# Merging two kinds of small product stages in a hybrid decoder kernel, and modelling its PSUM ring in the planner

## The chip, the cores and the metric

The kernel runs on one core of one Trainium2 chip, alone. The metric is the device time of one execution in microseconds, as the median of several runs. A profile comes from one execution on the chip. Its span goes from the first to the last instruction of that execution; its time as a run is a little longer.

## The reference, cut to what matters

Two layers of a decoder over 256 tokens of width 1024, all in fp32. A layer has one combined projection, two token mixers side by side, a gated merge, a convolution FFN and a gated embedding term:

```python
u = rms_norm(h, g_mix_norm)
qa, ka, va, qi, ki, wi, qb, kb, vb, gate_a, gate_b = split(u @ w_in)
# mixer A: 8 heads of 64, one key/value head, keys chosen by an indexer of 4 heads
rel = relu(einsum('bthd,bsd->bths', qi, ki))
iscore = where(causal, einsum('bths,bth->bts', rel, wi), -inf)
sel = top_k(iscore, 64)
o_a = softmax(qa . k_sel / 8, over valid keys) . v_sel
# mixer B: 4 heads, two softmax maps each
o_b = (softmax(q1 . k1 / 8) - lam * softmax(q2 . k2 / 8)) . vb
o_b = rms_norm(o_b, g_subln) * (1 - lam_init)
mix = sigmoid(gate_a) * (o_a @ w_branch_a) + sigmoid(gate_b) * (o_b @ w_branch_b)
h = h + mix @ w_out
h = h + conv_ffn(rms_norm(h))
h = h + sigmoid(rms_norm(h) @ w_ple_gate) * (p @ w_ple_proj)
```

The heads' queries and keys are RMS-normalised over their 64 elements (qa, ka, qb, kb) and rotated.

## The kernel before, in words

**The stream.** Every weight matrix comes in as 128 chunks of 128 x 1024 per layer, loaded by SyncE's queue into five raw buffers. ACT rounds a chunk to a high part (`split_hi`, L164) and DVE subtracts to get a low part (`split_lo`, L179; in the later part of the up-projection half of it is done on GpSimd, L175 and L176). A projection (`gemm_a`, L337 to L369) multiplies 128-row tiles of the activations, which also have a high and a low part, with both parts of the weights: three products (L361) of 512 columns for each k-step and each of the two token tiles. These products, those of the up-projection (L831, L833) and of the down-projection (L932 to L934) are most of PE's work, and they are written one after the other through the whole kernel. `prepare` (L199) splits chunks some way ahead of their use.

**The side work.** Whatever the mixers do is written as generators ("threads") and laid between the products by a planner, `Side` (L61 to L107). Each `yield` names what the stage that was just written costs on PE, DVE and ACT, in planner microseconds. `tick` (L83) is called every four token-tile steps of a projection (2.6 planner us of PE). It goes through the threads by priority, and resumes each one that is due: its last stage must be over by the planner's clocks plus a lag, DVE's clock may be at most `LIMIT_US` (3.5) ahead of PE's, and after `SIDE_US` (2) of PE time no further thread is resumed in this tick. `until` (L102) ticks with no products between, where the next product needs the side work. Then `prepare` splits further chunks. The order that the planner gives is the order of the instructions in each engine's queue; nothing is reordered by it on the chip.

**The threads of a layer.** `index_side` (L493) rotates the indexer's queries and keys, transposes them (L515, L431), and then, in one stage for each of the two query tiles i, multiplies them (L528, pairs of 64-row products, two PSUM buffers) and evicts with Relu (L531). It then spawns `select_side` (L536), which sums the heads' scores and finds the 64 largest on DVE in eight rounds (L551, L553; two rounds to a stage), which gives the mask for mixer A. `heads_side` (L568) normalises and rotates qb, kb and qa. `mixer_b` (L641) and `mixer_a` (L687) run once for each of two halves of the heads (hq) and two query tiles (i), in the orders `ORDER_B` and `ORDER_A`. A mixer's first stage is `maps` (L592): the mask is put into two PSUM buffers by an identity product (L602), the scores are added by 64-row products (L634 for B, L639 for A), DVE takes the row maxima (L607, L608), and ACT takes eight or four exponentials with their sums (L611). Then come a combination on DVE, transposes (`ptrans`, L626, L627), and the products with the values: L662 for B, which are evicted after a norm (L667 to L675), and L705 for A, four separate stages in a layer, each of which evicts to a high part (ACT, L709) and a low part (DVE, L710).

**PSUM.** Eight buffers: four for the projections (`ps_acc`, L118), and a ring of four for everything else (`ps_tp`, L119): transposes, index scores, maps, value products, and the up-projection's accumulators. A taker waits on the chip until the buffer's previous readers are done, and behind it all of PE's queue.

**Powers.** `rpow` (L260) gives (src * mul + add) ** -0.5 on GpSimd in two instructions, a tensor_scalar (L263) and a power (L264). `head_ss` (L417) squares on ACT (L420) and sums on DVE (L421).

**Between the layers.** `nxt_side` (L970) transposes and splits the first half of the new residual for the next layer while the second half's gate projection runs (`split_T_side`, L329; `split_T2`, L305, transposes at L317, evictions at L320 and L321). The residual itself is made by `gate` (L954: ACT L959, DVE L960 and L961). The next layer's `mid` (L458) does the second half.

Of the kernel before, what the change touches and what calls it, by code (L numbers as in the profile page):

```python
# [9 lines left out]
F32 = mybir.dt.float32  # L10
# [7 lines left out]
P = 128  # L18
L = 256
# [25 lines left out]
MA, MB = 0.9, 0.9  # L45
ORDER_A = [(0, 1), (1, 1), (0, 0), (1, 0)]
# [13 lines left out]

class Side:  # L61
# [6 lines left out]
    def __init__(self):  # L68
        self.threads = []
        self.pe = self.dve = self.act = 0.0  # L70

    def spawn(self, gen, prio=1):
        self.threads.append([prio, gen, 0.0])
        self.threads.sort(key=lambda t: t[0])
# [8 lines left out]
    def tick(self):  # L83
        start = self.pe
        for t in list(self.threads):
            if t[2] > self.pe or self.dve > self.pe + LIMIT_US or self.pe > start + SIDE_US:
                continue
            try:
                pe, dve, act = next(t[1])
            except StopIteration:  # L90
                self.threads.remove(t)
                continue
            self.pe += pe
            end = self.pe
            if dve:
# [14 lines left out]
def decoder_kernel(ctx: ExitStack, tc: tile.TileContext, x, xa, pT, ws, fc, tb, gf, rope, out):  # L110
# [149 lines left out]
    def rpow(dst, src, mul, add):  # L260
        n = src.shape[-1]
        t = sm.tile([P, 8], F32, name="pw", bufs=4)
        nc.gpsimd.tensor_scalar(t[:, :n], src, mul, add, op0=ALU.mult, op1=ALU.add)  # L263
        nc.gpsimd.tensor_tensor(dst, t[:, :n], mhalf[:, :n], op=ALU.pow)  # L264
# [18 lines left out]
    def b4(name, dt=F32):  # L283
        return blk.tile([P, 4, L], dt, tag="blk", name=name)

# [19 lines left out]
    def split_T2(srcs, hf, k0, scale, x, between=None, first=0):  # L305
# [5 lines left out]
        for a in range(0, 2, n):  # L311
            pt = ps_tp.tile([P, 2, L], F32, name="tp")[:, :n, :]
# [104 lines left out]
    def head_ss(src, n):  # L417
        sq = sm.tile([P, 8, 64], F32, name="sq", **T2)[:, :n, :]
        ss = sm.tile([P, 8], F32, name="hss", bufs=3)
        nc.scalar.activation(sq, src, AF.Square)  # L420
        nc.vector.reduce_sum(ss[:, :n], sq, axis=AX.X)  # L421
        return ss[:, :n]

    def transposed(srcs, nb, dst):

        for b0 in range(0, nb, 2):
            n = min(2, nb - b0)
            pt = ps_tp.tile([P, 2, L], F32, name="tp")
# [19 lines left out]
    for l in range(DEPTH):  # L448
# [44 lines left out]
        def index_side(pi):  # L493
            kk, iq, wvs = [], [], []
            for i in range(2):
# [6 lines left out]
                rpow(rk, head_ss(v[:, 0:64].unsqueeze(1), 1), 1.0 / 64, EPS)  # L502
# [9 lines left out]
            pt = ps_tp.tile([P, 2, L], F32, name="tp")  # L512
# [9 lines left out]
            for i in range(2):  # L522
                S = P * (i + 1)
                rel = b4("rel")[:, :, :S]
                ps = [ps_tp.tile([P, 2, L], F32, name="tp") for _ in range(2)]
# [7 lines left out]
                yield 0.85 * (i + 1), 0.0, 0.9  # L533
# [34 lines left out]
        def heads_side(pr, nm, is_q):  # L568

            rows, rq = [], []  # L570
            for i in range(2):
# [4 lines left out]
                if is_q:  # L576
                    rope_rows(q3, v, 8, rt[nm], i)
                    rpow(r_, head_ss(v, 8), 1.0, 64 * EPS)
                else:
                    rpow(r_, head_ss(v, 8), 1.0 / 64, EPS)  # L580
# [11 lines left out]
        def maps(qn, product, i, hq, mk):  # L592
# [6 lines left out]
            pss = [ps_tp.tile([P, 2, L], F32, name="tp") for _ in range(2)]  # L599
# [16 lines left out]
        def ptrans(src, nh, i):  # L616
# [4 lines left out]
            for a in range(0, n, 4):  # L621
                w = min(4, n - a)
                pt = ps_tp.tile([P, 4, P], F32, name="tp")
# [17 lines left out]
        def mixer_b(hq, i):  # L641
            while not {"qb", "kb"} <= flags:
                yield NONE
            pe, sums = maps("qb", product_b, i, hq, cmb)
            yield 0.9 + 0.9 * i, 0.8 + 0.6 * i, MA + MB * i
# [429 lines left out]
```

## Time and profile before

| what | value |
|---|---|
| time, median of 3 runs | 789.85 us (788.91 to 790.34) |
| the profiled execution's own time | 788.69 us |
| its span, first to last instruction | 786.9 us |
| around the span | 1.8 us |
| granted TensorE clock, mean over the span | 0.999 of full speed |
| PE matmul instructions | 4034 |
| read from HBM | 138.22 MB |

The profiled execution lies 0.2 us below the fastest of the three runs shown and 1.16 us below their median. In the profile, PE is TensorE's products, PEld its weight loads (which overlap them), DVE is VectorE, ACT ScalarE, POOL GpSimd and SP SyncE. A product's end in the trace is modelled and overlaps its successor's start, so the starts of successive products are what shows PE's pace; a merged row of a timeline gives the start of its first and the end of its last instruction. "Idle before" and its releaser stand in square brackets.

### The profile page before, as it was taken

The numbers are of one execution on the slowest core, as the hardware profiler recorded it, in microseconds if no ns is written. First come the engines' busy times: TensorE is split into PE (matmuls) and PEld (weight loads), VectorE is DVE, ScalarE is ACT, GpSimd is POOL, SyncE is SP. The second block draws the span as 40 slices with busy tenths as digits, with TensorE's granted clock in tenths as the row PEclk, the third lists the DMA queues.
The fourth block names the chain that finished last, engine by engine and source line by source line (L and its number), as shares of the span: only waits on it lengthen the run. The fifth ranks groups of instructions, "written<-read, shape, count | busy, mean of one in ns | idle before, by whom it ended". The sixth has DMA issues, their size and how long they took to land.

```text
span 786.9 us, 11698 instructions
## 1 busy us (share of the span) xinstructions
PE 779.7 (99%) x4034; PEld 648.1 (82%) x4034; DVE 588.6 (75%) x1128; ACT 501.3 (64%) x886; POOL 162.7 (21%) x162
## 2 busy tenths in 40 slices
PE   9999999999999999999999999999999999999997
PEld 7877886788888888888888778778888888888886
DVE  5987997675887778754687889768668878795643
ACT  5776657455877777553576486565468777773541
POOL 0250300001344442000123213000104444400000
PEclk9999999999999999999999999999999999999999
DMA  9654353462665556656465345445636656558521
GB/s 331 229 174 152 123 193 125 149 228 94 213 211 180 198 192 210 229 162 224 134 195 177 125 142 166 147 135 189 209 119 207 204 176 202 180 180 290 172 96 54
DMA packets 40204, 140.04 MB, mean 178 GB/s; under 512 B 4560, under 2 KB 5200, under 8 KB 40144
## 3 DMA queue, kind: packets, MB, share of 16 engines
q1 hardware_dynamic: 39280, 137.44, 52.8%
q10 hardware_dynamic: 864, 1.84, 0.7%
q8 instruction: 32, 0.52, 0.3%
q14 instruction: 28, 0.23, 0.1%
HBM read 138.22 MB, written 1.05 MB: 177 GB/s over the span
## 4 chain that ended last, share of the span: by engine, by line
PE 91%; DVE 3%; ACT 3%; POOL 1%; issue 1%; DVEq 0%; ACTq 0%
PE acc L361 36%; PE tp L831 21%; PE tp L833 11%; PE acc L932 5%; PE acc L934 5%; PE acc L933 5%; ACT pe L611 2%; PE tp L317 2%; DVE wl L179 2%; PE tp L626 1%; PE tp L705 1%; PE tp L662 1%; PE tp L639 1%; POOL rq L264 1%; PE tp L431 1%
## 5 line engine op out<-in xcount | busy, mean ns | idle before, releaser
L164 ACT ACTIVATE wh<-raw 128x1024 fp32r<-128x1024 f32 x254 | 263.9, 1057 | 38.4 <-PE acc L934 23.4
L179 DVE TENSOR_TENSOR wl<-raw,wh 128x1024 fp32r<-128x1024 f32 x178 | 213.8, 1220 | 27.8 <-ACT wh L164 27.5
L361 PE MATMUL acc<-wh,u 128*128 128x512 f32 (+1 forms) x672 | 215.1, 394 | 0.0
L831 PE MATMUL tp<-u,wh 128*128 128x512 f32 x704 | 177.1, 392 | 0.0
L361 PEld LDWEIGHTS acc<-wh,u 128*128 128x128 f32 x672 | 126.3, 189 | 26.7 <-issue 0.7
L831 PEld LDWEIGHTS tp<-u,wh 128*128 128x128 f32 x704 | 126.3, 189 | 22.3
L361 PE MATMUL acc<-wl,u 128*128 128x512 f32 (+1 forms) x336 | 129.3, 389 | 0.2 <-DVE wl L179 0.2
L176 POOL TENSOR_TENSOR wl<-raw,wh 128x512 fp32r<-128x512 f32 x76 | 98.5, 1296 | 142.8 <-ACT wh L164 60.9
L833 PEld LDWEIGHTS tp<-u,wl 128*128 128x128 f32 x704 | 96.6, 190 | 7.2
L833 PE MATMUL tp<-u,wl 128*128 128x256 f32 x704 | 98.8, 282 | 0.0
L865 DVE SCALAR_TENSOR_TENSOR cv<-tp,fc,cv 128x255 f32<-128x255 f32 (+1 forms) x176 | 84.2, 478 | 3.1
L361 PEld LDWEIGHTS acc<-wl,u 128*128 128x128 f32 x336 | 63.1, 188 | 12.5 <-DVE wl L179 1.0
L860 DVE TENSOR_TENSOR tp<-tp,cl 128x256 f32<-128x256 f32 x88 | 38.0, 432 | 45.8 <-ACT cl L858 45.4
L932 PE MATMUL acc<-wh,g 128*128 128x512 f32 x176 | 68.9, 391 | 0.0
L934 PE MATMUL acc<-wh,g 128*128 128x512 f32 x176 | 68.5, 389 | 0.0
L933 PE MATMUL acc<-wl,g 128*128 128x512 f32 x176 | 68.5, 389 | 0.0
L861 ACT ACTIVATE cv<-tp,fc 128x256 f32<-128x256 f32 x88 | 49.7, 565 | 25.8 <-DVE tp L860 25.3
L278 POOL TENSOR_SCALAR sst<-ss 128x2 f32<-128x2 f32 (+1 forms) x8 | 5.6, 698 | 259.8 <-ACT junk L270 259.6
L175 DVE TENSOR_TENSOR wl<-raw,wh 128x514 fp32r<-128x514 f32 x76 | 53.6, 705 | 0.0
L858 ACT ACTIVATE cl<-tp 128x256 f32<-128x256 f32 x88 | 33.6, 382 | 28.7 <-PE tp L833 28.6
L611 ACT ACTIVATE pe<-tp,nb,rq 128x256 f32<-128x256 f32 (+1 forms) x64 | 31.8, 528 | 18.0 <-DVE nb L608 12.2
L361 PE MATMUL acc<-wh,o 128*128 128x512 f32 x128 | 42.5, 399 | 0.0
(174 smaller groups left out, 946.4 us busy)
## 6 DMA issues: line engine op xcount, KB each, us to landing
raw<-ws SPq DMA_DIRECT2D x254, 512.0 KB, 3.5
raw<-ws SPq DMA_DIRECT2D x4, 256.0 KB, 5.1
h<-x SPq DMA_DIRECT2D x2, 512.0 KB, 7.1
gb<-gf ACTq DMA_DIRECT2D x2, 512.0 KB, 4.7
out<-h SPq DMA_DIRECT2D x3, 256.0 KB, 2.0
x<-xa SPq DMA_DIRECT2D x2, 256.0 KB, 3.9
px<-pT ACTq DMA_DIRECT2D x2, 256.0 KB, 2.7
tbl<-tb SPq DMA_DIRECT2D x1, 256.0 KB, 6.9
```

What stands on the lines that cost most here:

```text
L164: nc.scalar.activation(wh, raw, AF.Copy)
L175: nc.vector.tensor_sub(wl[:, a], raw[:, a], wh[:, a].bitcast(F32))
L176: nc.gpsimd.tensor_tensor(wl[:, b], raw[:, b], wh[:, b].bitcast(F32), op=ALU.subtract)
L179: nc.vector.tensor_sub(wl, raw, wh.bitcast(F32))
L361: nc.tensor.matmul(acc[i][:, :n], a, w, start=q == 0 and j == 0, stop=q == nk - 1 and not any(t[0] == i for t in todo[n_ + 1:]))
L831: nc.tensor.matmul(acc, wh[:, k, :], u.pair(k), start=k == 0, stop=False)
L833: nc.tensor.matmul(acc[:, 0, :], wl[:, k, :], u.hi(k), start=False, stop=k == KD - 1)
L861: nc.scalar.activation(c, pu, AF.Identity, bias=w[:, 3:4], scale=w[:, 2:3])
L865: nc.vector.scalar_tensor_tensor(c[:, sh:], pu[:, :L - sh], w[:, 2 - sh:3 - sh], c[:, sh:], op0=ALU.mult, op1=ALU.add)
L932: nc.tensor.matmul(acc[i], a, wh, start=k == 0, stop=False)
L933: nc.tensor.matmul(acc[i], a, wl, start=False, stop=False)
L934: nc.tensor.matmul(acc[i], b, wh, start=False, stop=k == NF - 1)
```

## The change

It does six things. (1) The two stages of index scores become one stage with one `yield`. (2) Mixer A's products with the values leave `mixer_a` and become a generator `values_a(i)`, which does both halves of the heads of a query tile in one stage, after both sets' transposes. (3) The planner keeps, for each of the four buffers of the ring, the time at which it should be free: after `BANK_US` in general, and after the exponentials (`EXP_US`, one after the other) for a set of maps. A thread that yields `Room(n)` is resumed only when the next n buffers are free by this reckoning; the two mixers' maps ask for two, mixer B's value products for one. (4) `rpow` is the power alone: the scale goes into ACT's square, the added epsilon becomes a tensor_scalar on DVE in `head_ss`, and in mixer B the epsilon is scaled by the squared sum of the exponentials (`es`), which saves three small multiplications and adds two small operations. (5) `nxt_side` first yields 2.8 us of DVE time without writing any instruction. (6) Every buffer of the ring is now taken through `tp`, which counts them.

The diff, without the hunks that only replace `ps_tp.tile(..., name="tp")` by `tp(...)`:

```diff
@@ -43,6 +43,8 @@
 MA, MB = 0.9, 0.9
+EXP_US = (1.75, 2.2)
+BANK_US = 0.9
 ORDER_A = [(0, 1), (1, 1), (0, 0), (1, 0)]
@@ -58,6 +60,13 @@
+class Room:
+    def __init__(self, n):
+        self.n = n
 class Side:
@@ -67,10 +76,14 @@
         self.threads = []
-        self.pe = self.dve = self.act = 0.0
+        self.pe = self.dve = self.act = self.exp = 0.0
+        self.free, self.taken = [0.0] * 4, 0
+    def room(self, n):
+        return all(self.free[(self.taken + j) % 4] <= self.pe for j in range(n))
     def spawn(self, gen, prio=1):
-        self.threads.append([prio, gen, 0.0])
+        self.threads.append([prio, gen, 0.0, 0])
         self.threads.sort(key=lambda t: t[0])
@@ -85,13 +98,27 @@
                 continue
+            if not self.room(t[3]):
+                continue
+            taken, t[3] = self.taken, 0
             try:
-                pe, dve, act = next(t[1])
+                got = next(t[1])
+                while isinstance(got, Room):
+                    t[3] = got.n
+                    got = next(t[1]) if self.room(got.n) else NONE
             except StopIteration:
...
                 continue
+            pe, dve, act, *exp = got
+            if got is not NONE:
+                t[3] = 0
             self.pe += pe
             end = self.pe
+            until = self.pe + BANK_US
+            if exp:
+                self.exp = until = max(self.exp, self.pe + LAG_US + dve) + exp[0]
+            for j in range(taken, self.taken):
+                self.free[j % 4] = until
             if dve:
@@ -257,11 +284,8 @@
-    def rpow(dst, src, mul, add):
-        n = src.shape[-1]
-        t = sm.tile([P, 8], F32, name="pw", bufs=4)
-        nc.gpsimd.tensor_scalar(t[:, :n], src, mul, add, op0=ALU.mult, op1=ALU.add)
-        nc.gpsimd.tensor_tensor(dst, t[:, :n], mhalf[:, :n], op=ALU.pow)
+    def rpow(dst, src):
+        nc.gpsimd.tensor_tensor(dst, src, mhalf[:, :src.shape[-1]], op=ALU.pow)
@@ -283,6 +307,11 @@
+    def tp(shape):
+        side.free[side.taken % 4] = side.pe + BANK_US
+        side.taken += 1
+        return ps_tp.tile(shape, F32, name="tp")
     class HL:
...
@@ -414,18 +443,20 @@
-    def head_ss(src, n):
+    def head_ss(src, n, scale, eps):
         sq = sm.tile([P, 8, 64], F32, name="sq", **T2)[:, :n, :]
         ss = sm.tile([P, 8], F32, name="hss", bufs=3)
-        nc.scalar.activation(sq, src, AF.Square)
+        nc.scalar.activation(sq, src, AF.Square, scale=scale)
         nc.vector.reduce_sum(ss[:, :n], sq, axis=AX.X)
+        nc.vector.tensor_scalar(ss[:, :n], ss[:, :n], eps, None, op0=ALU.add)
         return ss[:, :n]
...
             n = min(2, nb - b0)
-            pt = ps_tp.tile([P, 2, L], F32, name="tp")
+            pt = tp([P, 2, L])
             for j in range(n):
@@ -499,7 +530,7 @@
                 rk = sm.tile([P, 1], F32, name="rk")
-                rpow(rk, head_ss(v[:, 0:64].unsqueeze(1), 1), 1.0 / 64, EPS)
+                rpow(rk, head_ss(v[:, 0:64].unsqueeze(1), 1, 0.125, EPS))
                 iqi = sm.tile([P, 4, 64], F32, name="iq")
...
@@ -522,7 +553,7 @@
                 rel = b4("rel")[:, :, :S]
-                ps = [ps_tp.tile([P, 2, L], F32, name="tp") for _ in range(2)]
+                ps = [tp([P, 2, L]) for _ in range(2)]
                 for b in range(2):
@@ -530,7 +561,7 @@
                 rels.append(rel)
-                yield 0.85 * (i + 1), 0.0, 0.9
+            yield 2.1, 0.0, 1.8
             side.spawn(select_side(rels, wvs), P_TOPK)
@@ -575,9 +606,9 @@
                     rope_rows(q3, v, 8, rt[nm], i)
-                    rpow(r_, head_ss(v, 8), 1.0, 64 * EPS)
+                    rpow(r_, head_ss(v, 8, 1.0, 64 * EPS))
                 else:
-                    rpow(r_, head_ss(v, 8), 1.0 / 64, EPS)
+                    rpow(r_, head_ss(v, 8, 0.125, EPS))
                     rope_rows(q3, v, 8, rt[nm], i)
...
@@ -641,12 +672,15 @@
                 yield NONE
+            yield Room(2)
             pe, sums = maps("qb", product_b, i, hq, cmb)
-            yield 0.9 + 0.9 * i, 0.8 + 0.6 * i, MA + MB * i
+            yield 0.9 + 0.9 * i, 0.8 + 0.6 * i, MA + MB * i, EXP_US[i]
             rcp = sm.tile([P, 2, 2], F32, name="rcp", bufs=4)
...
             nc.vector.scalar_tensor_tensor(cf, rcp[:, 1, :], nlam, sums[:, 0, :], op0=ALU.mult, op1=ALU.mult)
+            es = sm.tile([P, 2], F32, name="es", bufs=4)
+            nc.vector.scalar_tensor_tensor(es, sums[:, 0, :], EPS, sums[:, 0, :], op0=ALU.mult, op1=ALU.mult)
             for m in range(2):
@@ -655,7 +689,8 @@
             yield 0.25 + 0.25 * i, 0.0, 0.3 + 0.2 * i
-            po = ps_tp.tile([P, 4, P], F32, name="tp")[:, 0:2, :]
+            yield Room(1)
+            po = tp([P, 4, P])[:, 0:2, :]
             for m in range(2):
@@ -664,14 +699,11 @@
             for m in range(2):
-                nc.scalar.activation(sq[:, m, :], po[:, m, :], AF.Square, accum_out=ss_[:, m:m + 1])
-            r1 = rcp[:, 0, :]
-            for _ in range(2):
-                nc.vector.tensor_mul(ss_, ss_, r1)
+                nc.scalar.activation(sq[:, m, :], po[:, m, :], AF.Square, scale=P ** -0.5, accum_out=ss_[:, m:m + 1])
+            nc.vector.tensor_add(ss_, ss_, es)
             ff = sm.tile([P, 2], F32, name="ff")
-            rpow(ff, ss_, 1.0 / P, EPS)
+            rpow(ff, ss_)
             yield 0.4 * (i + 1), 0.5, 1.6
-            nc.vector.tensor_mul(ff, ff, r1)
             nc.vector.tensor_mul(ob[:, i, hq * 256:(hq + 1) * 256].rearrange("p (b c) -> p b c", c=P), po,
@@ -687,8 +719,9 @@
                 yield NONE
+            yield Room(2)
             pe, sums = maps("qa", product_a, i, hq, mask[i])
-            yield 0.9 + 0.9 * i, 0.8 + 0.6 * i, MA + MB * i
+            yield 0.9 + 0.9 * i, 0.8 + 0.6 * i, MA + MB * i, EXP_US[i]
             rcp = sm.tile([P, 2, 2], F32, name="rcp", bufs=4)
@@ -697,19 +730,32 @@
             yield 0.5 + 0.5 * i, 0.0, 0.5 + 0.5 * i
+            pts[hq, i] = pt
+        pts = {}
+        def values_a(i):
+            while not {(0, i), (1, i)} <= set(pts):
+                yield NONE
             nb = i + 1
-            ptv = pt[:, :4 * nb, :].rearrange("p (m r s) t -> p m r s t", r=2, s=nb)
-            po = ps_tp.tile([P, 2, L], F32, name="tp")[:, 0, :].rearrange("p (m t) -> p m t", t=P)
-            for sb in range(nb):
-                for r in range(2):
-                    nc.tensor.matmul(po[r * 64:(r + 1) * 64], va[:, sb, :], ptv[:, :, r, sb, :],
-                                     start=sb == 0, stop=sb == i)
+            pos = []
+            for hq in range(2):
+                ptv = pts[hq, i][:, :4 * nb, :].rearrange("p (m r s) t -> p m r s t", r=2, s=nb)
+                po = tp([P, 2, L])[:, 0, :].rearrange("p (m t) -> p m t", t=P)
+                for sb in range(nb):
+                    for r in range(2):
+                        nc.tensor.matmul(po[r * 64:(r + 1) * 64], va[:, sb, :], ptv[:, :, r, sb, :],
+                                         start=sb == 0, stop=sb == i)
+                pos.append(po)
             x = o_parts()
-            hi, lo = x.two(2 * hq, slice(i * P, (i + 1) * P))
-            nc.scalar.activation(hi, po, AF.Copy)
-            nc.vector.tensor_sub(lo, po, hi.bitcast(F32))
-            yield 0.85 * nb, 0.4, 0.35
-            flags.add(("a", hq, i))
+            for hq in range(2):
+                hi, lo = x.two(2 * hq, slice(i * P, (i + 1) * P))
+                nc.scalar.activation(hi, pos[hq], AF.Copy)
+                nc.vector.tensor_sub(lo, pos[hq], hi.bitcast(F32))
+            yield 1.3 * nb, 0.8, 0.35
+            for hq in range(2):
+                flags.add(("a", hq, i))
@@ -733,6 +779,8 @@
             side.spawn(mixer_a(hq, i), 1)
+        for i in (1, 0):
+            side.spawn(values_a(i), 1)
...
@@ -968,6 +1016,7 @@
             def nxt_side():
+                yield 0.0, 2.8, 0.0
                 yield from split_T_side([h[:, i, HALF[0]] for i in range(2)], 0, lambda k: g_nxt[:, k:k + 1],
```

## Rows read from the trace of the kernel before

**Rows 1.** The page, section 1, whole run: engine, busy us (share), instructions.

```profile
PE 779.7 (99%) x4034; PEld 648.1 (82%) x4034; DVE 588.6 (75%) x1128; ACT 501.3 (64%) x886; POOL 162.7 (21%) x162
```

**Rows 2.** Waits of PE, whole run: total us, times, longest us.

```profile
PE tp L602 <- ACT pe L611: 0.9, 3, 0.5
...
PE tp L431 <- DVE qr L582: 0.2, 1, 0.2
```

**Rows 3.** Chain of waits, 45 to 56 us: start, length, what.

```profile
47.08 7.54 PE acc L361 x33
```

**Rows 4.** Timeline of PE, 41 to 42.5 us: start, length (modelled end), operation.

```profile
41.33 0.72 PE L528 MATMUL tp<-kiT,iqT 64*128 64x128 f32 x8
41.98 0.50 PE L361 MATMUL acc<-wh,u 128*128 128x512 f32 x1
42.31 0.39 PE L361 MATMUL acc<-wl,u 128*128 128x512 f32 x1
```

**Rows 5.** Timeline of PE, 145.3 to 146.9 us, last value product of layer 0.

```profile
145.37 0.39 PE L361 MATMUL acc<-wh,o 128*128 128x512 f32 x1
145.69 0.65 PE L705 MATMUL tp<-pt,va 128*64 128x256 f32 x4
146.27 0.50 PE L361 MATMUL acc<-wh,o 128*128 128x512 f32 x1
146.61 0.39 PE L361 MATMUL acc<-wl,o 128*128 128x512 f32 x1
```

**Rows 6.** Timeline of PE, 64.6 to 67.1 us, two sets of maps.

```profile
64.97 1.13 PE L634 MATMUL tp<-qT 64*128 64x256 f32 x8
66.04 0.39 PE L602 MATMUL tp<-cmb,identb 128*128 128x256 bf16 x2
66.36 0.72 PE L634 MATMUL tp<-qT 64*128 64x128 f32 x8
67.00 0.50 PE L361 MATMUL acc<-wh,u 128*128 128x512 f32 x1
```

**Rows 7.** Timeline of PE, three stretches with waits for PSUM.

```profile
69.90 0.59 PE L602 MATMUL tp<-cmb,identb 128*128 128x256 bf16 x2
...
71.49 0.28 PE L602 MATMUL tp<-cmb,identb 128*128 128x256 bf16 x1
...
72.19 0.71 PE L634 MATMUL tp<-qT 64*128 64x128 f32 x8
...
124.31 0.28 PE L602 MATMUL tp<-mk,identb 128*128 128x256 bf16 x1
...
125.27 0.71 PE L639 MATMUL tp<-kT,qT 64*128 64x128 f32 x8
...
480.94 1.16 PE L662 MATMUL tp<-prv,pt 128*128 128x128 f32 x8 [0.25 <-ACT qT L433]
```

**Rows 8.** GpSimd by line and form: count, busy, mean ns of one.

```profile
L264 POOL TENSOR_TENSOR rq<-pw,mhalf 128x8 f32<-128x8 f32 x12 | 22.8, 1899 | 1.0
L263 POOL TENSOR_SCALAR pw<-hss 128x8 f32<-128x8 f32 (+1 forms) x16 | 11.3, 708 | 99.5 <-DVE hss L421 79.5 <-DVE rcp L648 20.0
```

**Rows 9.** GpSimd's timeline; L507's durations (min/median/max), first and last start.

```profile
27.55 0.70 POOL L264 TENSOR_TENSOR rk<-pw,mhalf 128x1 f32<-128x1 f32 x1
...
L507 DVE TENSOR_SCALAR wv<-pri x4: 161/162/165, 28.2 to 415.4; 128x4 f32<-128x4 f32 x4
```

**Rows 10.** Timeline of PE, 386 to 390.5 us, transposes of the next layer's input.

```profile
386.44 0.93 PE L317 MATMUL tp<-ident,h 128*128 128x128 f32 x4
...
389.98 0.60 PE L317 MATMUL tp<-ident,h 128*128 128x128 f32 x4
```

**Rows 11.** Timelines: a low part's subtraction (DVE) and first product (PE).

```profile
82.34 1.22 DVE L179 TENSOR_TENSOR wl<-raw,wh 128x1024 fp32r<-128x1024 f32 x1
...
85.39 0.39 PE L361 MATMUL acc<-wl,u 128*128 128x512 f32 x1
```

**Rows 12.** Busy us (instructions) by engine in a window, DVE third.

```profile
80.00:100.00 20.00, 20.00 (x111) 16.94 (x110) 19.55 (x60) 13.35 (x30) 7.38 (x9) 1.00 0.40 132
```

More of the change, by code (lines that the diff above doesn't have):

```diff
@@ L311, in split_T2 @@
         for a in range(0, 2, n):
-            pt = ps_tp.tile([P, 2, L], F32, name="tp")[:, :n, :]
+            pt = tp([P, 2, L])[:, :n, :]
             pts.append(pt)
@@ L511, in index_side @@
                 yield 0.0, 2.8, 0.0
-            pt = ps_tp.tile([P, 2, L], F32, name="tp")
+            pt = tp([P, 2, L])
             for j in range(2):
@@ L598, in maps @@
             pe = b4("pe")[:, :, :S]
-            pss = [ps_tp.tile([P, 2, L], F32, name="tp") for _ in range(2)]
+            pss = [tp([P, 2, L]) for _ in range(2)]
             mk2 = mk.unsqueeze(1).broadcast_to([P, 2, n])
@@ L622, in ptrans @@
                 w = min(4, n - a)
-                pt = ps_tp.tile([P, 4, P], F32, name="tp")
+                pt = tp([P, 4, P])
                 for j in range(w):
@@ L788, in ffn_T @@
             for k in (0, 2):
-                pt = ps_tp.tile([P, 4, P], F32, name="tp")[:, 0:2, :]
+                pt = tp([P, 4, P])[:, 0:2, :]
                 for j in range(2):
@@ L839, in products @@
                 made[c] = chunk(l, c)
-                acc = ps_tp.tile([P, 2, L], F32, name="tp")
+                acc = tp([P, 2, L])
                 part_products(c, acc, range(KD))
@@ L846, in products @@
                     made[c_] = chunk(l, c_)
-                accs = [ps_tp.tile([P, 2, L], F32, name="tp") for _ in cs]
+                accs = [tp([P, 2, L]) for _ in cs]
                 for ks in (range(KD // 2), range(KD // 2, KD)):
```

## The prediction

> **What bounds the kernel.** I read the page's engine times first, then PE's waits, the chain of waits, and PE's timeline in the mixer stages. PE is busy for 99% of the span [rows 1], and the chain is a row of products: 33 of a projection take 7.54 us, 0.228 us each [rows 3]. DVE, ACT and GpSimd work beside it. So the time moves only by what leaves PE's own row or is put into it, and there are two such things here: what PE loses around small groups of products, and its waits for a PSUM buffer [rows 2]. 0.2% of the time (1.6 us) is about what a measurement of this kernel can tell from no change.
>
> **What one small group costs.** A set of maps shows eight products of 64 rows, which start in pairs: from 64.97 to 66.04 (1.07 us) at 256 columns and from 66.36 to 67.00 (0.64 us) at 128 [rows 6]. The 128 further columns of four pairs cost 0.43 us, 0.107 us a pair. The first group of index scores is four pairs of 128 columns: 0.43 us of work, but 0.65 us from its start to the next projection product, and that product holds PE for 0.33 us in place of 0.228 [rows 4]. The projection product before such a group also lasts longer, 0.32 us (145.37 to 145.69) [rows 5]. So a group loses 0.09 us on the way in, 0.22 inside and 0.10 on the way out: 0.41 us in all. A value group of two pairs of 256 columns needs 0.43 us and takes 0.58 (145.69 to 146.27), with 0.09 before and 0.11 after it (0.34 in place of 0.228) [rows 5]: 0.35 us.
>
> **Merged stages.** The same products are issued, in fewer groups. Index scores: two groups become one in each of two layers, 2 x 0.41 = 0.8 us. Values: four become two in each layer, 4 x 0.35 = 1.4 us; but three of the four groups of a layer are followed at once by transposes, where the 0.11 on the way out is not surely paid, so the low end is 4 x 0.24 = 1.0, and I take 1.2. Together 2.0 us, between 1.8 and 2.2. What the merging delays: the first value pair waits for the second set's transposes, and the last pair gives all of its parts to the branch product at once. Today the last group of layer 0 stands directly ahead of that product [rows 5]. Followed by hand through layer 0, the planner's constants bring the top-k rounds forward (below), start the maps of mixer A about two ticks earlier and end the values ahead of the last tick, so the gap stays covered. Without that cover PE would wait for a copy and a subtraction.
>
> **Room in PSUM.** The two mask products of an undisturbed set start 0.32 us before its 64-row products (66.04 to 66.36) [rows 6]. At 71.49 this takes 0.70 us, at 124.31 it takes 0.96, and at 69.90 the two seeds last 0.59 us in place of 0.39 [rows 6, 7]: 0.38, 0.64 and 0.20 us lost, because the buffer's exponentials on ACT are not done. The second layer repeats the first and the third of these. The value product at 480.94 waits 0.25 us [rows 7]. The sum is 0.38 + 0.64 + 0.20 + 0.38 + 0.20 + 0.25 = 2.05 us. With the change, two sets that start at planner time t have their buffers free at t + 5.65 and t + 7.4 (1.8 + 0.25 + 1.4 + 2.2; then 1.75 more), while the next tick is at t + 5.3: mixer B's second pair of sets is held until the tick after that, and in mixer A the fourth set alone is held for a tick. I take all 2.05 us as saved, since a held set starts 2.6 us of products later than one that was short of at most 0.64. Holding adds a group of its own for each single set, 0.1 to 0.2 us in each layer: 0.3 us back. Behind a held thread nothing queues, since the planner goes to the next thread; DVE receives a top-k pair of rounds in its place.
>
> **New waits.** Transposes and the merged stages take PSUM buffers without asking for room. The trace of before cannot show them in their new places; the bounds are 0 and all of today's 2.05 us coming back there. I take 0.5 us, one and a half waits like that at 71.49, nearer to zero because only the sets of maps hold a buffer through eight exponentials.
>
> **Powers alone on GpSimd.** Twelve first steps of 0.71 us leave GpSimd's chain ahead of the power of 1.90 us [rows 8], and four small ones per layer in mixer B. PE waited for such a chain once, 0.2 us at the transposes of kb [rows 2]; I take 0.2 (0 to 0.2). DVE receives 16 additions of the kind that takes 0.162 us [rows 9], 2.6 us in two layers; in mixer B 24 small operations leave DVE and 16 come. The low parts that DVE makes are its only work with a due time for PE, and the closest in the full stretch [rows 12] is ready at 83.56 for a product at 85.39, 1.83 us early [rows 11]. The additions lie well within it: nothing.
>
> The Trainium skill ("SBUF — State Buffer", section "Who interferes with whom") says that a VectorE tensor_scalar in a two-port mode and a GpSimd instruction shut each other out for the whole of an instruction, whichever came first. By that rule an added addition could wait for the other tile's power; the trace disagrees so far, since the tensor_scalar of L507 that began at 28.2, inside a power that ran from 27.55 to 28.25, took no longer than its fellows (161 to 165 ns) [rows 9]. It is the fourth rival.
>
> **The delayed split for the next layer.** Transposes at 386.44 last 0.93 us where the next four last 0.60 [rows 10]: 0.33 us of waiting for the residual, which goes. But the second pair moves to the layer's last tick, behind the last residual additions on DVE, and the next layer's third k-step needs it 2.5 us later. Bounds: 0.33 saved, or the same 0.33 lost there as well; I take 0.
>
> **Sum.** -2.0 - 2.05 + 0.3 + 0.5 - 0.2 = -3.45 us. The profiled execution took 788.69 us, so it would take 785.24. It stands 1.16 us under the median of the runs shown (789.85); with that added the forecast is 786.4 us, 0.44% less.
>
> **Rivals.** (a) Room pays nothing: waits of ACT's own making move with the sets, and only the merging counts: -2.0 + 0.3 + 0.5 = -1.2, 788.7 us. For it: the planner's exponentials are guesses, and ACT ran behind at 124.31. Against it: the hold is longer than each wait that it replaces. 0.14.
> (b) The merged stages empty the ring of four: the index stage takes all four buffers at once, and the next taker waits for the Relus. The nearest price is the longest wait of today, 0.64 us [rows 7]; one after each of the three merged stages of both layers, 6 x 0.64 = 3.8 in place of the 0.5 above, gives -0.1: 789.7 us. Against it: the planned 2.1 us of the index stage end its tick, so that 2.6 us of products follow before another taker. The Trainium skill ("TensorEngine Tiling (Array Packing)", "Gotcha 1: PSUM Pressure") warns of this, that row tiles need PSUM banks of their own; no row shows it for a merged stage. 0.08.
> (c) Slower: DVE becomes the bound. Held sets let pairs of top-k rounds (2.2 us by the planner) ahead of low parts where DVE is busy 19.55 of 20 us [rows 12] and the lead is 1.83 us [rows 11]. One pair costs 2.2 - 1.8 = 0.4 us, two cost 2.6 and three 4.8 in each layer; it decides from two pairs on: 2 x 2.6 gives +1.75, 791.6 us, and three 796.0. Against it: by the planner's constants one pair per layer moves, to a place ahead of that stretch, and leaves it lighter. 0.08.
> (d) The port rule holds: in each layer the second kb addition waits for the first tile's power, 1.9 us less the 0.7 saved, and PE's transposes with it: 2 x 1.2 = 2.4 us, -0.85 with the 0.2 lost too: 789.0 us. 0.04.
>
> **Numbers.** The forecast has 0.66, 786.4 us. Its own best end is -2.2 - 2.05 - 0.2 - 0.33 = -4.8, 785.1 us; an execution's spread around the median (0.5 to 0.9 us in the runs shown) takes the low end to 784.3. The high end takes in (a), (d) and the edge of (b): 789.4. Faster by over 0.2%: the forecast, and of (a) a part, since 788.7 is just inside the bound: 0.73. Within 0.2%: most of (a), (b) and (d), and a forecast whose new waits are all of 2.05: 0.19. Slower: (c): 0.08.
>
> **What would show it.** One group of sixteen L528 products per layer, directly one after the other; two value groups per layer; no idle time at L602 behind ACT's exponentials; no GpSimd tensor_scalar on the heads; PE's busy share unchanged, its projection rows shifted forward by some 3.5 us. I am wrong if waits at transposes or value products appear that sum to over 2 us, if low parts arrive late between 80 and 100 us, or if a value group again stands directly ahead of the branch product with PE idle behind it.

## The result, and the profile after

| | median | lowest to highest | ratio to before, 95% interval |
|---|---|---|---|
| before | 789.91 us | 788.91 to 790.34 (4 runs) | |
| after | 799.80 us | 798.73 to 801.38 (4 runs) | 1.0131 (1.0119 to 1.0144) |

The change makes the kernel 1.3% slower, outside the predicted range (784.3 to 789.4 us) and with the wrong sign. The profiled execution of after has a span of 796.8 us against 786.9: 9.9 us more.

Parts 1 and 2 of the page of after:

```profile
PE 779.6 (98%) x4034; PEld 649.6 (82%) x4034; DVE 589.9 (74%) x1136; ACT 501.1 (63%) x886; POOL 157.5 (20%) x138
...
PE   9999999999999999999999989899999999999997
```

PE issues the same 4034 products and is as long busy as in [rows 1]. What is new are slices below 9 in the middle: slices 24 and 26 of 40, at 458 to 478 and 498 to 518 us, the mixers of layer 1. PE's waits say behind what (engine, tile, line waited for; us in total, times, longest):

```profile
PE tp L657 <- ACT pe L642: 4.6, 4, 2.9
PE tp L633 <- ACT pe L642: 2.5, 1, 2.5
PE tp L462 <- DVE qr L613: 1.4, 1, 1.4
PE acc L167 <- DVE mhalf L158: 1.0, 1, 1.0
PE tp L633 <- ACT pt L658: 0.9, 1, 0.9
PE acc L390 <- DVE wl L206: 0.9, 2, 0.7
PE tp L657 <- DVE pe L728: 0.6, 1, 0.6
PE tp L657 <- DVE pe L685: 0.4, 1, 0.4
PE tp L657 <- ACT qT L464: 0.3, 1, 0.3
PE acc L390 <- ACT wh L218: 0.2, 1, 0.2
```

L633 is the mask product (L602 of before), L657 the transposes (L626), L642 the exponentials (L611), L638 and L639 the row maxima (L607, L608), L582 the top-k rounds (L551), L462 and L613 the heads' transposes and rows (L431, L582), L658 the eviction of transposes (L627), L685 and L728 the combinations on DVE (L651, L695). Without the 1.0 us at the very start, which both kernels have, the list sums to 11.8 us; the same view of before sums to 1.5 (the 0.9 and 0.2 of [rows 2], and two more of 0.2). That is 10.3 us more. By place, PE's timeline puts 1.4 us at kb's transposes and 2.2 at mixer B's transposes in layer 0, 2.9 at mixer B's transposes and 4.2 in mixer A's stages in layer 1, and 1.1 at high and low parts that came late. Counted by the starts of the same projection products in both traces, after falls 2.1 us behind before in layer 0 and 7.8 in layer 1. The longest waits in PE's timeline:

```profile
59.42 0.98 PE L462 MATMUL tp<-ident,qr 128*128 128x128 f32 x7 [1.40 <-DVE qr L613]
...
475.86 1.78 PE L657 MATMUL tp<-ident,pe 128*128 128x128 f32 x6 [2.90 <-ACT pe L642]
...
500.80 0.38 PE L633 MATMUL tp<-mk,identb 128*128 128x512 bf16 x1 [2.54 <-ACT pe L642]
```

Why are exponentials late in mixer B of layer 1? In ACT's timeline of after they follow long idle times behind DVE's L639:

```profile
460.68 0.56 ACT L642 ACTIVATE pe<-tp,nb,rq 128x256 f32<-128x256 f32 x1 [7.49 <-DVE nb L639]
...
474.61 0.56 ACT L642 ACTIVATE pe<-tp,nb,rq 128x256 f32<-128x256 f32 x1 [5.36 <-DVE nb L639]
```

DVE's timeline of after shows what stands ahead of the maxima, and the second block, from before, what stood there then:

```profile
450.98 0.61 DVE L582 MAX8 m<-sc 128x8 f32<-128x128 f32 x2
...
453.33 2.35 DVE L206 TENSOR_TENSOR wl<-raw,wh 128x1024 fp32r<-128x1024 f32 x2
455.60 0.61 DVE L582 MAX8 m<-sc 128x8 f32<-128x128 f32 x2
...
457.94 1.22 DVE L206 TENSOR_TENSOR wl<-raw,wh 128x1024 fp32r<-128x1024 f32 x1
459.08 1.29 DVE L638 TENSOR_REDUCE mx<-tp 128x2 f32<-128x512 f32 x2
...
462.48 0.61 DVE L582 MAX8 m<-sc 128x8 f32<-128x128 f32 x2
...
473.03 1.28 DVE L638 TENSOR_REDUCE mx<-tp 128x2 f32<-128x512 f32 x2
```

```profile
451.40 1.28 DVE L607 TENSOR_REDUCE mx<-tp 128x2 f32<-128x512 f32 x2
...
456.71 1.29 DVE L607 TENSOR_REDUCE mx<-tp 128x2 f32<-128x512 f32 x2 [1.82 <-PE tp L634]
...
462.38 0.61 DVE L551 MAX8 m<-sc 128x8 f32<-128x128 f32 x2
```

Before, the first pair's maxima ran at 451.40, straight after the maps on PE, and top-k began after both pairs, at 462.38. After, PE ended the first pair's maps at 456.49, but two top-k stages (450.98 and 455.60) were already in the queue, and the maxima ran at 459.08. The second pair's, held by Room to 464.83 on PE, waited for a third stage (462.48), qa's rotation and the first pair's combinations, until 473.03. The first pair's transposes take the second pair's buffers in the ring, which its exponentials still read: PE stood 2.90 us.

The wait of 2.54 us at 500.80, in mixer A, has another ground. DVE's timeline of after there:

```profile
497.96 1.29 DVE L638 TENSOR_REDUCE mx<-tp 128x2 f32<-128x512 f32 x2 [1.81 <-PE tp L670]
...
504.81 0.42 DVE L707 TENSOR_TENSOR ob<-tp,ff 128x256 f32<-128x256 f32 x1
```

DVE had been idle for 1.81 us when PE ended the first set, so no top-k stood in the way of its maxima. But mixer A's maps now come three ticks (36 projection products) earlier than in before, while mixer B's last values keep their tick. The last value product of mixer B still held its buffer of the ring: its eviction (L707) stands behind these maps in DVE's queue and ran at 504.81. So the second set had to wait for a buffer of the first, that is, for the first set's exponentials. This is read from the trace; no run tests it by itself.

A wait also cost something behind it. Windows of after (stretch, its length, PE, PEld, DVE, ACT, POOL, granted clock, DMA share, GB/s):

```profile
473.00:475.80 2.80, 0.00 (x0) 0.00 (x0) 2.73 (x8) 1.19 (x5) 0.00 (x0) 1.00 0.57 187
475.90:477.80 1.90, 1.84 (x7) 1.42 (x8) 1.89 (x4) 1.90 (x9) 0.00 (x0) 0.52 0.21 37
477.90:479.20 1.30, 1.30 (x5) 1.01 (x4) 0.62 (x1) 1.30 (x5) 0.00 (x0) 0.50 0.80 315
479.20:482.00 2.80, 2.80 (x14) 2.33 (x12) 1.80 (x3) 2.80 (x5) 0.86 (x1) 0.96 0.02 9
```

Behind the wait of 2.90 us the granted clock was about half, the 1.2 GHz level, for 3.2 us: 1.90 x 0.48 + 1.30 x 0.50 = 1.6 us of products lost. The account: 10.3 of waits + 1.6 of clock - 2.1 of merging (0.9 + 1.2, measured below) = 9.8 us, where the spans differ by 9.9. What holding's own groups cost (0.3 by the prediction) is not told apart in this.

### The profile page after: what moved, and what is told of

It is laid out like the page before. It is cut to its first block, busy times and chain, and to the rows that moved or that the text cites. A ratio compares the mean times of both kernels' runs of the same rounds, so it can differ in the third digit from the quotient of the medians.

```text
span 796.8 us, 11676 instructions
## 1 busy us (share of the span) xinstructions
PE 779.6 (98%) x4034; PEld 649.6 (82%) x4034; DVE 589.9 (74%) x1136; ACT 501.1 (63%) x886; POOL 157.5 (20%) x138
## 4 chain that ended last, share of the span: by engine, by line
PE 84%; DVE 9%; ACT 4%; issue 1%; POOL 1%; DVEq 0%; ACTq 0%; POOLq 0%
PE acc L390 31%; PE tp L879 20%; PE tp L881 11%; PE acc L980 5%; PE acc L982 5%; PE acc L981 5%; DVE wl L206 3%; ACT pe L642 2%; PE tp L346 1%; DVE mx L638 1%; PE tp L748 1%; PE tp L670 1%; ACT wh L191 1%; PE tp L657 1%; DVE hss L451 1%
## 5 line engine op out<-in xcount | busy, mean ns | idle before, releaser
L390 PE MATMUL acc<-wh,u 128*128 128x512 f32 (+1 forms) x672 | 216.0, 395 | 0.2 <-ACT wh L218 0.2
L390 PEld LDWEIGHTS acc<-wh,u 128*128 128x128 f32 x672 | 126.4, 189 | 28.6 <-issue 2.1
L390 PE MATMUL acc<-wl,u 128*128 128x512 f32 (+1 forms) x336 | 129.7, 390 | 0.9 <-DVE wl L206 0.9
L390 PEld LDWEIGHTS acc<-wl,u 128*128 128x128 f32 x336 | 63.4, 189 | 13.3 <-DVE wl L206 1.9
L642 ACT ACTIVATE pe<-tp,nb,rq 128x256 f32<-128x256 f32 (+1 forms) x64 | 31.8, 513 | 34.4 <-DVE nb L639 31.5
L288 POOL TENSOR_TENSOR rq<-hss,mhalf 128x8 f32<-128x8 f32 x12 | 26.6, 2219 | 95.3 <-DVE hss L452 74.7
```

Source lines behind the costliest of these rows:

```text
L390: nc.tensor.matmul(acc[i][:, :n], a, w, start=q == 0 and j == 0, stop=q == nk - 1 and not any(t[0] == i for t in todo[n_ + 1:]))
```

## The experiments

Four theories stood at the start. T1: top-k rounds let forward stand in DVE's queue ahead of the row maxima, so exponentials are late, PSUM buffers too, and PE waits. T2: the hold (`Room` keeps a thread back) does it, which puts the second pair just ahead of transposes that take its buffers. T3: a merged group costs by itself. T4: the powers. T5 came after the first eight runs: the merged index stage moves the order of everything behind it. All kernels compute the whole reference. The medians of before were 788.55 to 788.67 us in these sets, 1.3 us below the 789.91 of the first table. The expectations of the first two groups below were stated from the higher level, so it is differences from before and ratios that can be held against them.

**One part of the change at a time, on the kernel before.** idx_only:

```diff
                 rels.append(rel)
-                yield 0.85 * (i + 1), 0.0, 0.9
+            yield 2.1, 0.0, 1.8
```

> The kernel before with the one-stage index scores alone. Price of the merge by the prediction: 2 x 0.41 us less, so 789.1 us if nothing else moves. T1 (top-k rounds that run ahead of the maps' row maxima on DVE make the exponentials late, and with them the PSUM buffers): in layer 1 the planner lets two pairs of rounds out before the maxima of mixer B, as in the kernel after, so the stage of the maps in layer 1 costs PE 2 to 6 us and the time is 791 to 795 us; layer 0 stays as before. T2 (the hold of the second pair of map sets does it): no hold here, so 789 us. T3 (merged stages empty the ring): one wait of 0.6 us or so behind the merged stage in each layer, 790 us.

Measured: 796.91 us, 1.0113 (1.0095 to 1.0131). This edit of planner figures and grouping alone carries most of the loss: 8.3 us over before, more than any theory gave. PE's waits in it:

```profile
PE tp L602 <- ACT pe L611: 3.7, 4, 2.4
PE tp L602 <- DVE o L321: 2.0, 1, 2.0
PE tp L431 <- DVE qr L582: 1.6, 1, 1.6
PE tp L705 <- ACT pt L627: 1.1, 1, 1.1
```

T1's wait is there, 3.3 us at mixer B's masks in layer 1. But 3.6 us are waits in mixer A's stages of layer 1, which T1 did not name, and 1.6 us are for kb's rows in layer 0.

val_only takes `values_a` alone (part 2 of the change).

> The kernel before with the merged value stage of mixer A alone. By the prediction 1.2 us less in sum, 788.7 us. T1 and T2: nothing of the early part of a mixer moves, so 788.2 to 789.9 us with no new PE wait over 0.5 us. T3 (merged stages by themselves cost): the value groups wait for the second set's transposes or give all of their parts to the branch product at once, PE shows 1 us or more of idle time in each layer ahead of the branch product, 791 us or more.

Measured: 787.39 us, 0.9984 (0.9974 to 0.9993): 1.2 us less, as predicted, and no T3.

room_only takes `Room`, `tp` and the exponentials' figures (part 3).

> The kernel before with the planner's PSUM ring alone (sets of maps and mixer B's values ask for room; nothing merged). The prediction's terms give -2.05 + 0.3 + 0.5 = -1.25 us, 788.7 us. T2 (the held pair lands just ahead of the first pair's transposes, which take its buffers without asking): the hold and the 5.3 us to the first transposes are as in the kernel after, so 2.5 us or more of new waits at the transposes or at sets of mixer A in each layer, 794 to 800 us. T1 (top-k rounds ahead of the maxima): the hold lets only one single stage of rounds forward, so about half of the loss at most, 790 to 794 us, and the waits follow map sets whose maxima stand behind top-k on DVE.

Measured: 789.97 us, 1.0018 (1.0008 to 1.0027): 1.4 us more. That is not the gain predicted and far from T2's 4 us and more. As a difference from before it lies in T1's range, and in this kernel's layer 1 too a top-k stage stands ahead of the second pair's maxima on DVE. PE's waits in it have none left at the mask product (L602 of before), and new ones at transposes: 1.6 and 0.4 at mixer B's (L658), 0.5 at mixer A's values (L740).

pow_only takes the powers (part 4).

> The kernel before with only the powers left on GpSimd (scales in the squares, epsilons added on DVE). By the prediction -0.2 us, 789.7 us. T1 and T2: the planner's figures are the same, so the order is the same and the time within 0.2%, 788.3 to 791.5 us. T4 (the powers or DVE's additions cost by themselves): 791.5 us or more, with PE waiting for qr rows in each layer.

Measured: 788.60 us, 1.0001 (0.9992 to 1.0010). T4 falls.

**One part undone, on the kernel after.** after_no_room (`room` returns True):

> The kernel after, but every question for room is answered with yes, so no set is held (merged stages and powers stay). T2 (the hold is the cause): the loss goes, 787 to 790 us. T1 (top-k rounds ahead of the maxima): in layer 1 two pairs of rounds still stand ahead of the maxima of mixer B because of the one-stage index scores, so layer 1 still loses 3 to 6 us; layer 0 loses its 2.8 us no longer: 791 to 796 us.

Measured: 798.48 us, 1.0124 (1.0109 to 1.0139), as slow as after. T2 falls as the cause of the 10 us; T1's range was too low.

after_idx_split (the two index stages are back, all else stays):

> The kernel after with the index scores in two stages again (one tick later, top-k rounds one tick later). Merging itself gives back 0.8 us, so nothing else moving it is 800.6 us. T1: one stage of rounds in place of two stands ahead of the maxima, most of the loss goes, 790 to 794 us. T2: the held pair still lands 5.3 us ahead of the first pair's transposes in both layers, so the loss stays, 797 to 801 us.

Measured: 788.46 us, 0.9997 (0.9987 to 1.0006). The loss is gone with the hold still there. T2 falls again; T1 gave too small a relief.

after_topk_held:

```diff
+            while len(b_maps) < 4:
+                yield NONE
             m8 = [sm.tile([P, 8], F32, name=f"m8{i}", bufs=1) for i in range(2)]
...
             pe, sums = maps("qb", product_b, i, hq, cmb)
+            b_maps.append((hq, i))
```

> The kernel after, with the top-k rounds kept back until all four map sets of mixer B are issued; the hold of the second pair stays, 5.3 us ahead of the first transposes. T1: the maxima are no longer late, PE waits for PSUM buffers fall under 3 us in sum, 787 to 791 us, unless the rounds that then end later delay the mask of mixer A. T2: the hold and the distance are as in the kernel after, the 2.9 us and 2.5 us waits stay, 797 us or more.

Measured: 794.56 us, 1.0079 (1.0062 to 1.0095). A miss for both: top-k ahead of the maxima is a part, not all. Mixer A's waits are gone too: its maps stand three ticks later than in after, where before has them. PE still waited 3.3 us in two places for kb's rows (L462 <- qr) and 4.7 us at mixer B's transposes.

after_room_dve:

```diff
-                self.exp = until = max(self.exp, self.pe + LAG_US + dve) + exp[0]
+                self.exp = until = max(self.exp, max(self.dve, self.pe + LAG_US) + dve) + exp[0]
...
+            yield Room(1)
             pt = ptrans(pe[:, 0:4:2, :], 2, i)
...
+            yield Room(i + 1)
             pt = ptrans(pe, 4, i)
```

> The kernel after with the planner's ring told the truth at two places: a set's exponentials start after what is planned on DVE, and transposes ask for room too. T2 (takers that do not ask): the waits at transposes go and turn into holds, 787 to 791 us. T1: the top-k rounds still stand ahead of the maxima, the mixers' chain is as late, but PE does products of the projections in place of waiting: 790 to 796 us, with the PE waits behind ACT's exponentials under 4 us in sum and waits of the last stages in their place.

Measured: 797.50 us, 1.0104 (1.0084 to 1.0123), above both ranges. The 2.9 and 2.5 us waits stayed: asking did not help here, where DVE ran later than the planner's clock of it.

**What in the index stage?** In layer 0 of before, the planner was told 0.85 in one tick and 1.7 in the next, and the 1.7 with qb's next stage filled that tick (`SIDE_US` is 2), so kb's heads began a tick later. Told 2.1 in the first tick, the planner has that second tick free: in idx_only kb's heads and mixer B's maps come a tick (12 projection products) earlier on PE. In layer 1 the same figures do something else. There the first sums of the indexer's scores (L541), which stood behind kb's first row on DVE (438.59 in before), come ahead of it (430.43 in idx_only); top-k comes two stages ahead of mixer B's maxima; and kb's transposes and mixer B's maps come a tick later on PE, not earlier. Why the planner chose so in layer 1 was not followed step by step. idx_topk_held is idx_only with the edit of after_topk_held:

> The kernel before with the one-stage index scores issued at their early tick, and the top-k rounds kept back until all four map sets of mixer B are issued. Layer 0 is as in idx_only (+0.4 us at its end, with a 1.6 us wait of the kb transposes). T1 (rounds ahead of the maxima): layer 1's 2.4, 0.8 and 2.0 us waits behind ACT's exponentials go, what stays is a wait for kb's rows of 1.5 to 2 us in layer 1 too: 790 to 791.5 us. If the early maps alone were the cause, 794 us or more.

Measured: 791.08 us, 1.0035 (1.0022 to 1.0048), inside T1's range. With top-k held, kb's transposes and the maps of both mixers stand at the ticks of before again in layer 1. So early top-k, with all that it moves, costs idx_only 796.91 - 791.08 = 5.8 us: it is the exponentials behind late maxima in mixer B, and mixer A's stages that come two ticks earlier. PE's waits in idx_topk_held:

```profile
PE tp L431 <- DVE qr L585: 3.6, 2, 2.0
...
PE tp L605 <- ACT pe L614: 0.4, 2, 0.2
```

What remains is the other half of the order, 3.6 us for kb's rows in two places, where before waits 0.2 [rows 2]. In layer 0 (1.63 us) kb's transposes come a tick earlier on PE, while kb's rows are not made as much sooner on ACT, DVE and GpSimd. In layer 1 (1.99 us) the transposes stand where they stood, and kb's rows come later on DVE, behind the sums of the scores.

idx_late (an empty stage of 0.1 first, the merged group told as 1.9 a tick later) and after_idx_late (the same in after):

> The kernel before with all index scores in one group, issued one tick later (where the second of the two groups was), so that every later step keeps the tick it has in the kernel before. T5 (what costs is the order: the one-stage scores end a tick or more earlier in the planner, so kb's heads, the maps and the top-k rounds move against the products): the merge now pays its 0.8 us alone, 787.8 us (787.2 to 788.4), and no PE wait over 0.5 us that the kernel before does not have. T3 (the merged group itself empties the ring and costs): 794 us or more, as in idx_only.

> The kernel after with the merged index group issued one tick later. T5: the loss goes, -0.8 for the index group and -1.2 for the values (both as measured or predicted alone) and +1.4 for the ring (room_only): 788.0 us (787 to 789). T2 (the hold): 795 us or more, since the hold of the second pair stays in both layers.

Measured: 789.41 us, 1.0019 (1.0008 to 1.0030), and 789.26 us, 1.0011 (1.0001 to 1.0020). Most of the loss is gone, but idx_late is 1.6 us over its expectation. Its trace has a 1.62 us wait for kb's rows in layer 1: there the order had still moved (qb's transposes come two ticks later than in before). after_idx_late, 0.3 us over its range, has the same wait, 1.5 us long. late_no_room is after_idx_late with `room` always True:

> The kernel after with the merged index group one tick later and every question for room answered with yes: merged index group, merged values and powers, in the order of the kernel before. T5: 788.6 - 0.8 - 1.2 = 786.6 us (786.0 to 787.2), faster than both kernels. If room paid what the prediction took for it (1.75 us less its new waits), this would be slower than after_idx_late; by room_only it is 1.4 us faster.

Measured: 788.22 us, 0.9993 (0.9984 to 1.0002), with a wait of 1.5 us for kb's rows. 1.6 us over the expectation, as much as that wait.

**Every tick kept.** idx_same_order is idx_only with the figures of before, the work in the second stage:

```diff
+            yield 0.85, 0.0, 0.9
             rels = []
             for i in range(2):
...
-            yield 2.1, 0.0, 1.8
+            yield 1.7, 0.0, 0.9
```

> The kernel before with all index scores in one group, and the planner told the old costs of the two stages (0.85, then 1.7 with the work in the second), so that not one later step changes its tick. T5 (the order is the whole cost; the kb wait left in idx_late is one tick of h1qb and hkb in layer 1): 2 x 0.41 us less, 787.7 us (787.2 to 788.3), and the waits of the kernel before and no other over 0.5 us. T3 (the merged group costs something by itself): 788.5 us or more, with idle time of PE behind the group.

Measured: 787.70 us, 0.9989 (0.9980 to 0.9998). The same merged group that lost 8.3 us gains 0.9 when nothing behind it moves. T3 falls. after_same_order is after with this edit alone:

> The kernel after with nothing changed but the planner's costs and tick of the index scores (still one group on PE). T5: the 10 us loss goes whole and only the ring's own cost is left: 786.6 + 1.2 = 787.8 us (787.2 to 788.5). If part of the loss were the merged group or the hold: 790 us or more.

Measured: 787.58 us, 0.9987 (0.9978 to 0.9996): the whole loss goes by two planner figures and the tick of the merged group. same_no_room has `room` always True as well:

> Merged index group with the old planner costs, merged values, powers; room always granted. T5: -0.8 and -1.2 us add up, 786.6 us (786.1 to 787.2), the fastest of all. If merged pieces hinder each other: 787.5 us or more.

Measured: 786.37 us, 0.9970 (0.9959 to 0.9981). same_room_ask has Room and the edits of after_room_dve:

> Merged index group with the old planner costs, merged values, powers, and the ring with both repairs (transposes ask too; exponentials counted from DVE's clock). If room costs because transposes do not ask: 786 to 787 us, with the 1.1 and 0.4 us waits at mixer B's transposes in layer 1 gone. If it costs because the held pair lands later and closer to what follows: 787.5 to 789 us.

Measured: 785.89 us, 0.9965 (0.9953 to 0.9978), 0.1 us under the range that was expected, and the fastest kernel here: 0.35% below before. It lies 1.7 us under after_same_order; from same_no_room its interval cannot tell it. PE's waits of after_same_order, then of same_room_ask:

```profile
PE tp L658 <- ACT pe L643: 1.8, 3, 1.1
...
PE tp L658 <- DVE pe L686: 0.4, 1, 0.4
PE tp L658 <- ACT qT L464: 0.3, 1, 0.3
```

```profile
PE acc L390 <- DVE wl L206: 1.6, 3, 0.7
...
PE tp L658 <- ACT pe L643: 0.3, 1, 0.3
```

The transposes (L658) no longer wait 2.5 us in sum but 0.3; 1.4 us come back as low parts that are late (L390 <- wl, 1.6 against 0.2).

## Why the prediction was wrong, point by point

**The bound** (PE's row; only waits and small groups count): right as far as it goes. The account above closes to 0.1 us with waits, groups and the clock behind a wait, which the prediction did not have. Of its own signs of being wrong the first came: waits at transposes, 5.9 us in sum in after.

**Price of a small group and merged stages, -2.0**: right. The merged index group of layer 0 in after:

```profile
41.27 0.39 PE L390 MATMUL acc<-wh,u 128*128 128x512 f32 x1
41.59 1.58 PE L559 MATMUL tp<-kiT,iqT 64*128 64x128 f32 x16
43.10 0.50 PE L390 MATMUL acc<-wh,u 128*128 128x512 f32 x1
```

From 41.59 to 43.10 are 1.51 us, for 1.28 us of work by 0.107 a pair of 128 columns (four such pairs and four of twice the width): one loss of 0.23 inside, not two. In runs: -0.9 for the index groups (0.8 taken), -1.2 for the values (1.2 taken).

**What the merging delays or moves: the step that failed.** The prediction says: "Followed by hand through layer 0, the planner's constants bring the top-k rounds forward (below), start the maps of mixer A about two ticks earlier and end the values ahead of the last tick, so the gap stays covered." The moves were booked as cover at a price of nothing, and layer 1 was not followed. For layer 0 the cover did hold: no wait in mixer A there. But the `yield` figures are not a description; they make the order. 2.1 in place of 0.85 and 1.7 moved kb's heads a tick earlier in layer 0, and in layer 1 put top-k two stages ahead of mixer B's maxima and mixer A's maps close behind mixer B's values. The price, idx_only against idx_same_order, is 796.91 - 787.70 = 9.2 us: 5.8 for early top-k and what it moves, 3.4 for kb's rows and the rest. That the order is the cause is shown by the runs; how the 5.8 divide between mixer B and mixer A is read from the waits of one trace.

**Rival (c)** had the sign and the queue, not the place: the argument against it, "by the planner's constants one pair per layer moves, to a place ahead of that stretch", was false in layer 1, where three stages came ahead of the second pair's maxima. Late were the maxima, and through them PSUM buffers, not low parts (0.9 us of all waits in after). Mixer A's share, 4.2 us in after, it did not have.

**Room, -2.05 + 0.3, and new waits, +0.5**: wrong in size and sign. The waits view of before has only 0.9 + 0.2 us at mask and value products; the 2.05 was read from the starts and lengths of rows, whose ends are modelled. The new waits in after_same_order are 1.8 + 0.4 + 0.3 = 2.5 us, above the upper bound of 2.05, all at transposes, which do not ask. 2.5 - 1.1 = 1.4 is the 1.2 to 1.4 us that Room costs in after_same_order against same_no_room and in room_only. The reason given for "nearer to zero", that only maps hold buffers long, was the reason for the opposite: it is the maps' buffers that the transposes take next. Asking there makes the gain at most 0.5 us (786.37 to 785.89). The saving was not empty: by the starts of the same projection products, after_same_order gains 1.0 us on same_no_room in layer 0 and loses 2.2 in layer 1, where the waits at transposes are.

**Powers, -0.2 and nothing on DVE**: the 0.2 us wait for kb's rows is gone in pow_only, but no time is measured. GpSimd's chain for a kb tile became shorter by 0.33 us, half of the 0.71 taken, which is a mean over two shapes [rows 8]; the step that went lasted 0.56 us there. Its rows around kb's first tile, in before and in pow_only:

```profile
50.49 0.56 POOL L263 TENSOR_SCALAR pw<-hss 128x8 f32<-128x8 f32 x1 [2.23 <-DVE hss L421]
51.14 1.69 POOL L264 TENSOR_TENSOR rq<-pw,mhalf 128x8 f32<-128x8 f32 x1
```

```profile
50.77 2.01 POOL L261 TENSOR_TENSOR rq<-hss,mhalf 128x8 f32<-128x8 f32 x1 [3.24 <-DVE hss L420]
```

2.34 us (50.49 to 52.83) became 2.01: the power by itself takes 0.32 us longer than in before. Rival (d), the port rule of the Trainium skill ("SBUF — State Buffer", "Who interferes with whom"), would have shown as a longer wait for kb's rows in pow_only; there is none. The trace's ground against it was thin, though: the tensor_scalar at 28.20 overlaps the power that ended at 28.25 by 0.05 us.

**The delayed split, 0**: in same_no_room the transposes that lasted 0.93 us [rows 10] last 0.60, and by the starts of the same products 0.2 us come back behind them. About 0.2 is left, inside the bounds.

**Rivals (a) and (b)**: (a), Room pays nothing, is near the truth with the order kept: after_same_order gains 1.0 us on before, where (a) has 1.2. (b): idx_same_order and val_only show no wait that a merged group causes.

That same_no_room measured 786.37 us, the forecast's 786.4, is chance: the forecast lies 3.45 us under a before of 789.85, same_no_room 2.25 us under one of 788.62. What can be compared are the terms: without Room and with the order kept, -2.0 for the merging and -0.2 for the powers stand against the 2.25 measured. The terms on PE's own row were right; the order was the error.

## What to carry to other kernels

Where a planner writes the order, an edit of a cost figure is an edit of every queue behind it: list the order before and after, for each layer, and for each step that comes earlier ask whether its inputs do too. A merge should first be made with the old figures in the old tick, so that its own price shows; here that was 0.9 us of gain against 8.3 us of loss. A model of a ring of buffers must count every taker, or the one that does not ask inherits the wait.

## What the runs showed of the hardware that was not expected

After the 2.90 us wait the granted clock was 0.50 to 0.52 for 3.2 us (windows above). In idx_only too: it stood at 0.52 from 462.2 to 464.0 us, after waits of 2.44 and 0.82 us; and in after_no_room at 0.50 from 460.0 to 466.0, around and behind waits of 2.40 and 0.72 us. But not after every wait of such length: in after, PE was busy for 0.25 us from 498.0 to 500.7, and from 500.9 to 503.0 the clock was 1.00:

```profile
498.00:500.70 2.70, 0.25 (x1) 0.10 (x1) 1.41 (x3) 1.16 (x5) 0.00 (x0) 1.00 0.19 79
500.90:503.00 2.10, 2.10 (x13) 1.39 (x13) 0.73 (x2) 0.94 (x4) 0.00 (x0) 1.00 0.00 0
```

GpSimd's power has no fixed price: 1899 ns on the mean before [rows 8] and 2294 in pow_only, for the same shapes. In these two traces its length goes with what DVE was doing when it began: 2.50 to 2.56 us in the ten that began during a low-part subtraction, 1.69 to 2.01 in the nine that began during a rotation, 1.64 in the five others.
